# A two-layer hybrid backbone: a projection tile tied to each chunk of the forward scan, in step with the chunk, its input given two chunks later

## The chip, the cores and the metric

One Trainium2 (trn2) chip, one core. The time is that of one execution on the device, in microseconds (us). Before the change three runs gave 2162.40, 2163.49 and 2163.54 us; the median, 2163.49 us, is the figure to be forecast for the changed kernel. The profile is of one further execution. A difference of under about 0.2% (4.3 us) can't be told from no change here.

## What is computed

```python
def ssd_chunked(x, dt, a, bm, cm, h0):          # chunks of 128 tokens
    ...
    y_diag = jnp.einsum('btlsgr,btsgrp->btlgrp', cb[..., None] * decay, xdt)
    ...
    def step(h, inp):
        s, d = inp
        return h * d[..., None, None] + s, h
    h_final, h_in = lax.scan(step, h0, (jnp.moveaxis(states, 1, 0), jnp.moveaxis(chunk_decay, 1, 0)))
    ...
    y_off = jnp.einsum('btlgn,btgrpn,btlgr->btlgrp', cc, h_in, jnp.exp(a_cum))
    return (y_diag + y_off).reshape(bsz, L, G, R, P).astype(x.dtype), h_final

# in ssd_branch: both directions, gate, norm
    y = y_f + fl(y_b) + xs * d_skip.reshape(SSD_GROUPS, SSD_HPG, 1)
    y = y.reshape(bsz, L, SSD_INNER)
    return rms_norm(y * jax.nn.silu(z), norm_w), h_f, h_b

# in reference, for each of the two layers
        x = layer_norm(DEEPNORM_ALPHA * x + g_x * y_x, ln_g[layer], ln_b[layer])
```

1280 tokens (256 of context, 1024 latent) of width 1024 go through two layers in fp32. Layer 0 has two branches side by side, a bidirectional Mamba-2 scan (SSD, 16 heads of 64) and a conformer convolution. Each gives 1024 columns, and one output projection takes both, `y_x = concat(ssd, conformer) @ w_out`. Layer 1 (gMLP and windowed attention) is not touched.

## The kernel before

**Tiles and products.** Tokens go in ten tiles of 128. An fp32 product of the projection is made of three TensorE products of rounded halves: high by high, high by low, low by high. A token tile's half of the projection is 8 slices of the inner dimension, by three products, by two column halves: 48 products of 128x512, all on line L1003 (`out_mm_`, which `yield`s after each). They are called fills here.

**Two halves of the projection.** `stage_b` projects the conformer half of a token tile (its input was written to DRAM long before), adds it to the scaled residual `xl` and stores the sum in `tb_d`. `stage_a` does the SSD half later, when all of the scan's output `wt_d` is to be had. The input of either is loaded by `out_y`: a DMA from SP's queue into `yl` (L991, one buffer), then ScalarE's cast to `yh` (L158) and GpSimd's difference to `ylo` (L159, two buffers each).

**The forward scan.** Ten chunks of 128 tokens, one object `SsdFwd` each. `prep` loads the chunk's rows (`xt2`), makes the new state (`Hf`, two products on L1577) and the pair `cb` (L1590). `mix` makes the chunk's output in `t3`. For each of two groups of heads there are two products `po` with the incoming states (L1624) and, twice over, a pair `sg` of 15-row products (L1635), a mask on VectorE, an exponential on ScalarE, a product with `cbs` on GpSimd into `dec` (L1641), and eight 64-column products `yd` (L1645). `finish` gates the output with `zst` on VectorE (L1652), takes its squares on ScalarE (L1655) and `rs` and `rstd` from them on GpSimd (L1547, L1548), and turns `zst` with two sets of four transposes (L1660) for the store to `wt_d`.

**What sets the order.** The program is written in the order of the loop below, but the framework schedules it (`TileContext(nc, schedule_with_timeline_sim=True)`): each engine's instructions are put in an order of the scheduler's own, and each engine then works through its own in that order, waiting at each for what it needs. Buffers that exist once (`t3`, `zst`, `yl`, `yd`, each `sg`, the bank of `po`) must be read out before they are written again.

```python
for c in range(NT):
    S[c].mix()
    if c < NT - 1:
        S[c + 1].prep()
    S[c].finish()
    self.stage_b((c + 2) % NT, ob, w, yb_d, tb_d, grow, y0 if c == 0 else None)
```

At chunk 4 and 7 the same loop starts loads of the next weights (`wa`, 512 KB each).

Of the kernel before, what the change touches and what calls it, by code (L numbers as in the profile page):

```python
# [14 lines left out]
P = 128  # L15
# [5 lines left out]
NT = T // P  # L21
# [69 lines left out]
def run(steps):  # L91

    for _ in steps:
        pass


def h16(t):
    return t.rearrange("p (h d) -> p h d", d=64)
# [12 lines left out]
class Kern:  # L111
# [114 lines left out]
    def layer0(self):  # L226
        tc, nc, A = self.tc, self.nc, self.A
# [8 lines left out]
        yb_d = {a: dram.tile([8, P, b - a], F32, name=f"yb{a}_d") for a, b in SLICES}  # L236
# [3 lines left out]
        tb_d = dram.tile([NT, P, D], F32, name="tb_d")  # L240
# [8 lines left out]
        with e1:  # L249
            with ExitStack() as e2:  # L250
# [14 lines left out]
                wb, wl, y0 = self.inproj0(hhi, hlo, cv, xbc_d, zs_d, gs_d, dtr, vwh, yb_d, xt_d, hb_d, s0, first)  # L265
# [9 lines left out]
        ob = eo.enter_context(self.pool(name="ob", bufs=2))  # L275
        self.px = e.enter_context(self.pool(name="px", bufs=1, space=PSUM))
        g0, g1 = (ob.tile([P, D], F32, name=n, bufs=1) for n in ("g0", "g1"))
        grow = (g0, g1)
        wb0 = ob.tile([P, D], F32, name="xl", tag="xl")
        nc.sync.dma_start(wb0, A["wout0"][8])  # L280
        w = self.split_wo(wo, wb + [(0, wb0, None)], [(wl, "wb0")])
# [4 lines left out]
        with ExitStack() as e3:  # L286
            q = e3.enter_context(self.pool(name="sf", bufs=2, side="right"))
            self.rows = q.tile([111, 1280], FR, name="rows", bufs=1)
            self.rst = q.tile([111, 1280], F32, name="rst", bufs=1)
            nc.gpsimd.memset(self.rst, 0.0)  # L290
            for z in range(0, 128, 32):
                nc.sync.dma_start(self.rst[z:z + 12, :1024], A["delta"][0:12, :1024])
                nc.sync.dma_start(self.rst[z + 12:z + 15, 1024:], A["delta"][12:15, :256])
            self.mku = q.tile([P, P], mybir.dt.uint8, name="mku", bufs=1)
            nc.vector.tensor_copy(self.mku, self.tu)
            self.mmt = ("m0", "m1")
            self.ko = (*range(1, 8), 0)
            S = [SsdFwd(self, c, xbc_d, xt_d, hb_d, zs_d, wt_d, rstd, q) for c in range(NT)]
            S[0].prep()
            for c in range(NT):  # L300
                S[c].mix()
                if c < NT - 1:
                    S[c + 1].prep()
                S[c].finish()
                self.stage_b((c + 2) % NT, ob, w, yb_d, tb_d, grow, y0 if c == 0 else None)
                if c == 7:
                    wl3 = ea.enter_context(self.pool(name="wl3", bufs=1))
                    for k in range(4, 6):
                        wa.append((k, wl3.tile([P, D], F32, name=f"wa{k}", tag=f"wa{k}"), (wl3, f"wa{k}")))
                        nc.sync.dma_start(wa[k][1], A["wout0"][k])  # L310
                if c == 4:
                    for k in range(4):
                        nc.vector.tensor_copy(wa[k][1][:1, :1], self.Hf[:1, :1])
                        nc.sync.dma_start(wa[k][1], A["wout0"][k])
# [29 lines left out]
        for t in (*range(2, NT), 0, 1):  # L344
            ps = self.bank("mm")
# [638 lines left out]
        run(self.out_mm_(ps, parts or self.out_y(ob, src), w, by_k))  # L984
        return ps

    def out_y(self, ob, src):
        nc = self.nc
        oy = self.oy or ob
        y = oy.tile([P, 8, P], F32, name="yl", tag="yl", bufs=1)  # L990
        nc.sync.dma_start(y, src)  # L991
        hi = oy.tile([P, 8, P], FR, name="yh", tag="yh")
        lo = oy.tile([P, 8, P], FR, name="ylo", tag="ylo")
        self.split(y, hi, lo, self.oy is not None)
        return hi, lo
# [26 lines left out]
        nc.vector.scalar_tensor_tensor(rs[:, 1:2], mv[:, 0:1], -1.0, rs[:, 0:1], op0=ALU.mult, op1=ALU.mult)  # L1022
        return rs

    def stage_b(self, t, ob, w, yb_d, tb_d, grow, y0=None):
        nc, A = self.nc, self.A
        ts = slice(t * P, (t + 1) * P)
        x = ob.tile([P, D], F32, name="xl", tag="xl")
        nc.sync.dma_start(x, A["xc"][ts])
        a = max(x for x in yb_d if x <= t * P)  # L1030
        ps = self.out_mm(ob, yb_d[a][:, :, t * P - a:(t + 1) * P - a].rearrange("k p t -> p k t"), w, parts=y0, by_k=y0 is not None)
        g = grow[1 if t < 2 else 0]
        for f in range(2):
            fs = slice(512 * f, 512 * f + 512)
            u = ob.tile([P, 512], F32, name="u", tag="u", bufs=1)
            nc.vector.tensor_tensor(u, ps[f], g[:, fs], op=ALU.mult)
            nc.vector.scalar_tensor_tensor(x[:, fs], x[:, fs], ALPHA, u, op0=ALU.mult, op1=ALU.add)
        nc.sync.dma_start(tb_d[t], x)
# [512 lines left out]
class SsdFwd:  # L1551
# [51 lines left out]
    def mix(self):  # L1603

        K, c, q, nc = self.K, self.c, self.q, self.K.nc
        hb_d, zs_d = self.d[2:4]
        H, xt, bc, cb = self.H, self.xt, self.bc, self.cb
        zs = self.zs = q.tile([P, D], F32, name="zst", bufs=1)
        nc.sync.dma_start(zs, zs_d[c])
        t3 = q.tile([P, D], F32, name="t3", bufs=1)  # L1610
        nc.gpsimd.tensor_tensor(h16(t3), h16(xt[:, :D]), self.coef.rearrange("p g h -> p (g h)").unsqueeze(2).broadcast_to([P, 16, 64]), op=ALU.mult)
        self.t3 = t3
        for g in range(2):
            hs = slice(8 * g, 8 * g + 8)
            cs = slice(512 * g, 512 * g + 512)
            hb = None
            if c != 1:
                hb = q.tile([P, 512], F32, name="hbt", bufs=1)
                nc.sync.dma_start(hb, hb_d[c, :, cs])
            for d, S in ((1, hb), (0, H[:, cs] if H is not None else None)):  # L1620
                if S is None:
                    continue
                po = K.pp.tile([P, 512], F32, name="po", tag="m2", bufs=1)
                nc.tensor.matmul(po, bc[:, 2 + g], S, start=True, stop=True)  # L1624
                ea = K.expA[:, d, c, hs].unsqueeze(2).broadcast_to([P, 8, 64])
                t2 = q.tile([P, 512], F32, name="t2", bufs=1)
                nc.vector.tensor_tensor(h16(t2), h16(po), ea, op=ALU.mult)
                nc.vector.tensor_tensor(t3[:, cs], t3[:, cs], t2, op=ALU.add)
            yd = K.px.tile([P, 512], F32, name="yd", tag="yd", bufs=1)
            for j in range(2):  # L1630
                seg = []
                for d in range(2):
                    sg = K.px.tile([P, 512], F32, name=f"sg{d}", tag=f"sg{d}", bufs=1)
                    z = slice(64 * g + 32 * d, 64 * g + 32 * d + 15)
                    nc.tensor.matmul(sg, K.rows[z, 1024 + P * j:1024 + P * j + P], K.rows[z, 512 * j:512 * j + 512], start=True, stop=True)  # L1635
                    seg.append(sg)
                v4 = lambda t: t.rearrange("p (h t) -> p h t", h=4)
                nc.vector.copy_predicated(out=v4(seg[1]), mask=K.mku.unsqueeze(1).broadcast_to([P, 4, P]), data=v4(seg[0]))
                M = q.tile([P, 4, P], F32, name="dec", bufs=3)
                nc.scalar.activation(M.rearrange("p h t -> p (h t)"), seg[1], AF.Exp)  # L1640
                nc.gpsimd.tensor_tensor(M, M, cb[:, g * P:(g + 1) * P].unsqueeze(1).broadcast_to([P, 4, P]), op=ALU.mult)  # L1641
                for h in range(4):
                    o = 256 * j + 64 * h
                    for f in range(2):
                        nc.tensor.matmul(yd[64 * f:64 * f + 64, o:o + 64], M[:, h, 64 * f:64 * f + 64], xt[:, 512 * g + o:512 * g + o + 64], start=True, stop=True)  # L1645
            nc.vector.tensor_tensor(t3[:, cs], yd, t3[:, cs], op=ALU.add)

    def finish(self):

        K, c, q, nc = self.K, self.c, self.q, self.K.nc  # L1650
        w = self.zs
        nc.vector.tensor_tensor(w, self.t3, w, op=ALU.mult)  # L1652
        ssq = q.tile([P, 1], F32, name="ssq")
        wT = q.tile([P, D], F32, name="tmp", bufs=1)
        nc.scalar.activation(wT, w, AF.Square, accum_out=ssq)  # L1655
        K.rstd_of(ssq, self.rstd[:, c:c + 1], 1.0 / D)
        for g in range(2):
            ps = K.bank("ms")
            for k in range(4):
                nc.tensor.transpose(out=ps[:, k * P:(k + 1) * P], in_=w[:, 512 * g + k * P:512 * g + (k + 1) * P], identity=K.ident)  # L1660
            nc.scalar.copy(wT[:, 512 * g:512 * g + 512], ps)
        nc.sync.dma_start(self.d[4][c], wT.rearrange("p (k t) -> p k t", k=8))
# [19 lines left out]
```

## Time and profile before

| | |
|---|---|
| median of three runs | 2163.49 us |
| the profiled execution | 2159.51 us |
| its span, first to last instruction | 2157.5 us |
| PE (TensorE products) busy | 2050.3 us, 95% |
| PEld (weight loads, beside PE) busy | 1631.5 us, 76% |
| DVE (VectorE) busy | 1344.7 us, 62% |
| ACT (ScalarE) busy | 990.9 us, 46% |
| POOL (GpSimd) busy | 980.0 us, 45% |

The profiled execution is 2.0 us longer than its span, and 4.0 us shorter than the median. The forward scan runs from about 780 to 1058 us of the span.

### The profile page before, as it was taken

To read this page: it belongs to the slowest core of one execution; us is meant where nothing else is said; L and a number is where in the kernel's file an instruction comes from. 1 tells how busy PE (TensorE), PEld (TensorE's weight loads), DVE (VectorE), ACT (ScalarE), POOL (GpSimd) and SP (SyncE) were. 2 spreads that over 40 slices of the span, in tenths; PEclk is the share of its full clock that TensorE was granted. 3 is DMA by queue.
4 is the path that set the end of the run, shared out by engine and by line. 5 is a ranking of instruction groups with operands and counts; after the bars stand their busy time and mean duration, and the time that the engine had idled before them with its cause. 6 is when DMAs were issued, how large, how long until landed. Compare 5 with 4: busy or idle time off the path is not lost. (4 is left out here: it accounts for less than half of the span.)

```text
span 2157.5 us, 28255 instructions
## 1 busy us (share of the span) xinstructions
PE 2050.3 (95%) x10636; PEld 1631.5 (76%) x10636; DVE 1344.7 (62%) x1889; ACT 990.9 (46%) x1549; POOL 980.0 (45%) x646
## 2 busy tenths in 40 slices
PE   7999999999995999999899999999999998899896
PEld 6888888889873876665588788888777776677675
DVE  6788897758454335678776221422566766676676
ACT  7455667543362132224233333333666877655510
POOL 0198999800222235556421114823345555434562
PEclk9999999999996999999899999999999999999998
DMA  8011122235756645555343322522312111533463
GB/s 311 30 40 33 47 87 79 88 131 191 234 161 203 241 144 176 179 190 175 120 147 113 129 71 98 186 83 84 101 48 67 51 47 48 157 112 115 145 179 127
DMA packets 156976, 268.01 MB, mean 124 GB/s; under 512 B 18677, under 2 KB 97393, under 8 KB 156585
## 3 DMA queue, kind: packets, MB, share of 16 engines
q1 hardware_dynamic: 155416, 262.69, 37.0%
q0 software_dynamic: 1280, 3.26, 0.5%
q8 instruction: 83, 1.36, 0.3%
q14 instruction: 53, 0.43, 0.1%
q10 hardware_dynamic: 144, 0.26, 0.0%
HBM read 189.17 MB, written 76.94 MB: 123 GB/s over the span
## 5 line engine op out<-in xcount | busy, mean ns | idle before, releaser
L1236 POOL TENSOR_TENSOR accq<-accq,prod 128x1295 f32<-128x1295 f32 x90 | 287.7, 3197 | 33.9 <-ACT prod L1235 17.2
L171 PE MATMUL m<-hhi,wh 128*128 128x512 f32 (+1 forms) x792 | 280.9, 355 | 1.8 <-ACT th L1279 0.9
L171 PE MATMUL m<-hlo,wh 128*128 128x512 f32 (+1 forms) x792 | 280.6, 354 | 0.0
L171 PE MATMUL m<-hhi,wl 128*128 128x512 f32 (+1 forms) x792 | 280.2, 354 | 0.0
L1244 DVE SCALAR_TENSOR_TENSOR acc<-u,vwh,acc 128x1295 f32<-128x1295 f32 x150 | 235.1, 1568 | 12.9 <-ACT acc L1241 9.7
L171 PE MATMUL m<-h1hi,wh 128*128 128x512 f32 (+1 forms) x544 | 213.2, 392 | 1.7 <-ACT rb L423 1.4
L733 POOL TENSOR_TENSOR pl<-pt,ph 128x512 fp32r<-128x512 f32 x96 | 129.3, 1349 | 186.2 <-ACT ph L732 178.7
L171 PE MATMUL m<-h1lo,wh 128*128 128x512 f32 (+1 forms) x544 | 213.0, 392 | 0.0
L171 PE MATMUL m<-h1hi,wl 128*128 128x512 f32 (+1 forms) x544 | 212.1, 390 | 0.0
L1003 PE MATMUL m<-wol,yh 128*128 128x512 f32 x448 | 182.1, 406 | 1.3 <-DVE wol L956 1.1
L1003 PE MATMUL m<-woh,yh 128*128 128x512 f32 x448 | 181.4, 408 | 1.8 <-ACT yh L158 0.9
L1003 PE MATMUL m<-woh,ylo 128*128 128x512 f32 x448 | 182.0, 406 | 0.3 <-DVE ylo L159 0.3
L1235 ACT ACTIVATE prod<-u,vwh 128x1295 f32<-128x1295 f32 x90 | 124.1, 1381 | 97.9 <-POOL accq L1236 95.6
L171 PEld LDWEIGHTS m<-hhi,wh 128*128 128x128 f32 x792 | 149.7, 189 | 24.1 <-ACT th L1279 1.6
L171 PEld LDWEIGHTS m<-hhi,wl 128*128 128x128 f32 x792 | 149.7, 189 | 20.8
L171 PEld LDWEIGHTS m<-hlo,wh 128*128 128x128 f32 x792 | 149.8, 189 | 20.6
L159 POOL TENSOR_TENSOR wl<-wr,wh 128x1024 fp32r<-128x1024 f32 x33 | 81.5, 2471 | 117.2 <-ACT wh L158 95.2
L732 ACT CAST ph<-pt 128x512 fp32r<-128x512 f32 x152 | 93.1, 619 | 81.5 <-PE po L740 70.4
L740 PE MATMUL po<-ph,vs 128*66 128x512 f32 x304 | 122.0, 401 | 3.8 <-ACT yo L745 3.8
L171 PEld LDWEIGHTS m<-h1hi,wh 128*128 128x128 f32 x544 | 102.7, 189 | 22.9 <-ACT rb L423 2.0
L171 PEld LDWEIGHTS m<-h1hi,wl 128*128 128x128 f32 x544 | 102.6, 189 | 21.0 <-issue 0.2
L171 PEld LDWEIGHTS m<-h1lo,wh 128*128 128x128 f32 x544 | 102.8, 189 | 19.7
(371 smaller groups left out, 4765.6 us busy)
## 6 DMA issues: line engine op xcount, KB each, us to landing
wr<-in_wch_dram SPq DMA_DIRECT2D x69, 512.0 KB
mw<-in_modw_dram SPq DMA_DIRECT2D x24, 512.0 KB
mr<-in_modw_dram SPq DMA_DIRECT2D x16, 512.0 KB
wor<-in_wout_dram SPq DMA_DIRECT2D x16, 512.0 KB
xbc_d<-acc SPq DMA_DIRECT2D x12, 640.0 KB
xcT<-xbc_d SPq DMA_DIRECT2D x20, 320.0 KB
xt_d<-xtok SPq DMA_DIRECT2D x20, 320.0 KB
xtok<-xt_d SPq DMA_DIRECT2D x10, 640.0 KB
```

The costliest lines, as they stand in the source:

```text
L159: (nc.gpsimd if pool_lo else nc.vector).tensor_tensor(lo, src, hi.bitcast(F32), op=ALU.subtract)
L171: nc.tensor.matmul(out, x(k), y(k), start=(c == 0), stop=(c == tot - 1))
L732: nc.scalar.copy(ph, p)
L733: (nc.gpsimd if x in (0, 1, 3) else nc.vector).tensor_tensor(pl, p, ph.bitcast(F32), op=ALU.subtract)
L740: nc.tensor.matmul(po[:66], vs[:, kb, v], p[y], start=first and i == 0, stop=last and i == 2)
L1003: nc.tensor.matmul(ps[f], y[u][:, k], w[k][v][:, 512 * f:512 * f + 512], start=i + j == 0, stop=i + j == 9)
L1235: nc.scalar.activation(pr, u[:, k:k + N], AF.Copy, scale=vwh[:, i, k:k + 1])
L1236: nc.gpsimd.tensor_tensor(acc, acc, pr, op=ALU.add)
L1244: nc.vector.scalar_tensor_tensor(acc[:, :N], u[:, k:k + N], vwh[:, i, k:k + 1], acc[:, :N], op0=ALU.mult, op1=ALU.add)
```

## The change

The loop ties conformer tile i (token tile (i + 2) mod 10) to the scan. Tile 0 is given whole before chunk 0. Tile c + 1 is given with chunk c, four fills at each of the places where `mix` now yields (ahead of each `po`, each pair `sg` and each group `yd`: twelve, or ten where a state is missing), the rest behind it. The input of tile c + 2 is given with chunk c and is put behind the norm of chunk c - 1: a GpSimd copy of one element from that chunk's `rstd` into `yl` must end before the load may write there. So tile 3 waits for chunk 0, tile 4 for chunk 1, and so on to tile 9 and chunk 6; tiles 0 to 2 wait for none.

```diff
             S[0].prep()
+            run(self.stage_b(0, ob, w, tb_d, grow, y0))
+            ys = [self.stage_b_y(1, ob, yb_d)]
             for c in range(NT):
-                S[c].mix()
+                if c + 2 < NT:
+                    ys.append(self.stage_b_y(c + 2, ob, yb_d, S[c - 1] if c else None))
+                b = self.stage_b(c + 1, ob, w, tb_d, grow, ys.pop(0)) if c + 1 < NT else iter(())
+                for _ in S[c].mix():
+                    for _ in range(4):
+                        next(b, None)
+                run(b)
                 if c < NT - 1:
                     S[c + 1].prep()
                 S[c].finish()
-                self.stage_b((c + 2) % NT, ob, w, yb_d, tb_d, grow, y0 if c == 0 else None)
...
-    def out_y(self, ob, src):
+    def out_y(self, ob, src, behind=None):
         nc = self.nc
         oy = self.oy or ob
         y = oy.tile([P, 8, P], F32, name="yl", tag="yl", bufs=1)
+        if behind is not None:
+            nc.gpsimd.tensor_copy(y[:1, 0, :1], behind.last)
         nc.sync.dma_start(y, src)
...
-    def stage_b(self, t, ob, w, yb_d, tb_d, grow, y0=None):
+    def stage_b_y(self, i, ob, yb_d, behind=None):
+
+        t = (i + 2) % NT
+        a = max(x for x in yb_d if x <= t * P)
+        return self.out_y(ob, yb_d[a][:, :, t * P - a:(t + 1) * P - a].rearrange("k p t -> p k t"), behind)
+
+    def stage_b(self, i, ob, w, tb_d, grow, y):
...
-        ps = self.out_mm(ob, yb_d[a][:, :, t * P - a:(t + 1) * P - a].rearrange("k p t -> p k t"), w, parts=y0, by_k=y0 is not None)
+        ps = [self.bank("mm") for f in range(2)]
+        yield from self.out_mm_(ps, y, w, i == 0)
...
+                yield
                 po = K.pp.tile([P, 512], F32, name="po", tag="m2", bufs=1)
...
                 seg = []
+                yield
                 for d in range(2):
...
+                yield
                 for h in range(4):
...
         K.rstd_of(ssq, self.rstd[:, c:c + 1], 1.0 / D)
+        self.last = self.rstd[:1, c:c + 1]
```

In the changed program the same lines have other numbers: fills L1012, the load of `yl` L1000, `po` L1641, `sg` L1653, `yd` L1664, transposes L1680, state L1593, `cb` L1606, `rs` and `rstd` L1563 and L1564, `t3` L1627, `dec` L1659; the new copy is L999.

**Where instructions stand now.** The scheduler moves the fills among the chunks' own products. PE at the end of chunk 5, before: `zst_7684` is that chunk's gated output, and the fills around its transposes are of one and the same tile.

```order
L1003 MATMUL m1_8664<-woh7_6540,yh_8667 128x512
L1003 MATMUL m1_8664<-wol7_6541,yh_8667 128x512
L1660 MATMUL ms_7822<-cs_65,zst_7684 128x128 x4
L1660 MATMUL ms_7828<-cs_65,zst_7684 128x128 x4
L1645 MATMUL yd_7916<-xt2_7780,dec_7922 64x64 x8
L1003 MATMUL m1_8664<-woh7_6540,ylo_8668 128x512
L1003 MATMUL m1_8664<-woh0_6544,yh_8667 128x512
L1003 MATMUL m1_8664<-wol0_6545,yh_8667 128x512
```

After, at the same place, `zst_7766` is chunk 5's output and `yh_7979` the input of tile 8, whose load stands behind the norm of chunk 5:

```order
L1012 MATMUL m1_7992<-woh0_6544,ylo_7763 128x512
L1680 MATMUL ms_7963<-cs_65,zst_7766 128x128 x4
L1680 MATMUL ms_7969<-cs_65,zst_7766 128x128 x4
L1653 MATMUL sg1_8042<-rows_6579 128x512
L1664 MATMUL yd_8011<-xt2_7921,dec_8021 64x64 x8
L1653 MATMUL sg0_8086<-rows_6579 128x512
L1653 MATMUL sg1_8088<-rows_6579 128x512
L1012 MATMUL m0_8208<-woh1_6516,yh_7979 128x512
L1012 MATMUL m0_8208<-wol1_6517,yh_7979 128x512
L1012 MATMUL m1_8209<-woh1_6516,yh_7979 128x512
L1012 MATMUL m1_8209<-wol1_6517,yh_7979 128x512
```

The last fill of tile 7 now stands ahead of the transposes, and the first of tile 8 behind them and four own pieces.

PE at the end of chunk 7, before (`zst_8116`): all fills are over by then.

```order
L1645 MATMUL yd_8355<-xt2_8212,dec_8361 64x64 x8
L1660 MATMUL ms_8254<-cs_65,zst_8116 128x128 x4
L1660 MATMUL ms_8260<-cs_65,zst_8116 128x128 x4
L1635 MATMUL sg0_8402<-rows_6579 128x512
L1635 MATMUL sg1_8404<-rows_6579 128x512
L1590 MATMUL ms_8448<-bcT_8437 128x128 x2
L1635 MATMUL sg0_8418<-rows_6579 128x512
L1635 MATMUL sg1_8420<-rows_6579 128x512
```

After (`zst_8200`): `yh_8810` is the input of the first tile of `stage_a`, with that stage's weights.

```order
L1653 MATMUL sg0_8474<-rows_6579 128x512
L1680 MATMUL ms_8397<-cs_65,zst_8200 128x128 x4
L1641 MATMUL po_8440<-Hf_8144,bcT_8357 128x512
L1012 MATMUL m0_8806<-woh0_8755,yh_8810 128x512
L1012 MATMUL m1_8807<-woh0_8755,yh_8810 128x512
L1680 MATMUL ms_8403<-cs_65,zst_8200 128x128 x4
L1653 MATMUL sg1_8476<-rows_6579 128x512
L1012 MATMUL m0_8806<-wol0_8756,yh_8810 128x512
L1012 MATMUL m0_8806<-woh0_8755,ylo_8811 128x512
```

Fills now stand between the own products of chunks 7 and 8, where there were none.

POOL behind chunk 5, before (`rs_7819` and `rstdA` are that chunk's norm, `ylo_8881` belongs to `stage_a`):

```order
L1641 TENSOR_TENSOR dec_7922<-dec_7922,cbs_7806 128x512
L1547 TENSOR_SCALAR rs_7819<-ssq_7816 128x1
L1611 TENSOR_TENSOR t3_7902<-xt2_7780,coef_7812 128x1024
L1548 TENSOR_TENSOR rstdA_88<-rs_7819,mhalf_67 128x1
L1641 TENSOR_TENSOR dec_7938<-dec_7938,cbs_7806 128x512
L159 TENSOR_TENSOR ylo_8881<-yl_8878,yh_8880 128x1024
```

After, behind chunk 5 (the copy gives tile 8's buffer `yl_7976` free for its load):

```order
L1659 TENSOR_TENSOR dec_7898<-dec_7898,cbs_7722 128x512
L1563 TENSOR_SCALAR rs_7960<-ssq_7957 128x1
L1564 TENSOR_TENSOR rstdA_88<-rs_7960,mhalf_67 128x1
L999 COPY yl_7976<-rstdA_88 1x1
L1659 TENSOR_TENSOR dec_8021<-dec_8021,cbs_7947 128x512
L1627 TENSOR_TENSOR t3_7985<-xt2_7921,coef_7953 128x1024
L1659 TENSOR_TENSOR dec_8045<-dec_8045,cbs_7947 128x512
L159 TENSOR_TENSOR ylo_7980<-yl_7976,yh_7979 128x1024
```

And after, behind chunk 2, for tile 5 (`yl_7317`):

```order
L1563 TENSOR_SCALAR rs_7301<-ssq_7298 128x1
L1564 TENSOR_TENSOR rstdA_88<-rs_7301,mhalf_67 128x1
L1627 TENSOR_TENSOR t3_7326<-xt2_7262,coef_7294 128x1024
L1659 TENSOR_TENSOR dec_7362<-dec_7362,cbs_7288 128x512
L999 COPY yl_7317<-rstdA_88 1x1
```

The copy stands right behind the norm at chunk 5, and behind two larger pieces at chunk 2. What follows it in the row waits until the norm is done.

## Rows read from the trace of the kernel before

**Rows 1.** The page, section 1: busy time, share of the span, instructions.

```profile
PE 2050.3 (95%) x10636; PEld 1631.5 (76%) x10636; DVE 1344.7 (62%) x1889; ACT 990.9 (46%) x1549; POOL 980.0 (45%) x646
```

**Rows 2.** Windows: stretch, length, busy of PE, PEld, DVE, ACT, POOL, PEclk, DMA share, GB/s.

```profile
780.00:1060.00 280.00, 268.17 (x1522) 172.48 (x1521) 195.60 (x281) 90.29 (x131) 153.56 (x99) 0.97 0.52 173
```

**Rows 3.** Timeline of PE, end of the scan: start, duration, instruction, [idle before <-releaser].

```profile
1013.01 0.49 PE L1635 MATMUL sg<-rows 15*128 15x512 f32 x1
1013.43 1.09 PE L1660 MATMUL ms<-cs,zst 128*128 128x128 f32 x8
1014.45 0.69 PE L1645 MATMUL yd<-xt,dec 128*64 128x64 f32 x16
1015.07 0.74 PE L1635 MATMUL sg<-rows 15*128 15x512 f32 x2
...
1022.14 1.98 PE L1577 MATMUL ms<-tmp,xt 128*128 128x512 f32 x4
1023.97 1.02 PE L1624 MATMUL po<-Hf,bcT 128*128 128x512 f32 x2
1024.92 0.50 PE L1635 MATMUL sg<-rows 15*128 15x512 f32 x1
...
1042.72 0.49 PE L1645 MATMUL yd<-xt,dec 128*64 128x64 f32 x6
...
1052.60 1.58 PE L1624 MATMUL po<-hbt,bcT 128*128 128x512 f32 x2 [2.97 <-issue]
...
1058.41 0.50 PE L1003 MATMUL m<-woh,yh 128*128 128x512 f32 x1 [0.78 <-DVE t L1627]
```

**Rows 4.** Windows of that end, columns as in rows 2.

```profile
1052.00:1054.00 2.00, 1.40 (x2) 0.30 (x2) 1.93 (x3) 0.00 (x0) 2.00 (x2) 0.77 0.82 334
1054.00:1056.00 2.00, 1.59 (x27) 1.44 (x28) 1.74 (x3) 0.00 (x0) 0.12 (x1) 0.50 0.03 8
1056.00:1058.00 2.00, 1.63 (x13) 0.68 (x10) 0.33 (x1) 0.00 (x0) 0.00 (x0) 0.88 0.00 0
1028.00:1043.00 15.00, 13.98 (x86) 8.24 (x86) 12.00 (x22) 5.91 (x10) 7.37 (x8) 0.54 0.38 129
```

**Rows 5.** Timeline of PE: one own product among fills.

```profile
816.49 0.40 PE L1003 MATMUL m<-wol,yh 128*128 128x512 f32 x1
816.72 0.40 PE L1003 MATMUL m<-woh,ylo 128*128 128x512 f32 x1
817.05 0.49 PE L1635 MATMUL sg<-rows 15*128 15x512 f32 x1
...
817.80 0.40 PE L1003 MATMUL m<-wol,yh 128*128 128x512 f32 x1
```

**Rows 6.** Timelines of SP's queue and ACT: a load's issue, its cast.

```profile
807.50 0.38 SPq L991 DMA_DIRECT2D yl<-yb_d  x1
818.40 0.37 SPq L991 DMA_DIRECT2D yl<-yb_d  x1
...
814.60 1.05 ACT L158 CAST yh<-yl 128x1024 fp32r<-128x1024 f32 x1 [6.62 <-DMA yl<-yb_d]
823.34 1.05 ACT L158 CAST yh<-yl 128x1024 fp32r<-128x1024 f32 x1 [3.34 <-DMA yl<-yb_d]
```

**Rows 7.** Timeline of all engines: from a chunk's gate to its norm.

```profile
869.90 1.22 DVE L1652 TENSOR_TENSOR zst<-t,zst 128x1024 f32<-128x1024 f32 x1
871.15 1.06 ACT L1655 ACTIVATE tmp<-zst 128x1024 f32<-128x1024 f32 x1 [3.80 <-DVE zst L1652]
871.20 2.29 POOL L1611 TENSOR_TENSOR t<-xt,coef 128x1024 f32<-128x1024 f32 x1 [2.50 <-DVE zst L1652]
...
873.57 0.69 POOL L1547 TENSOR_SCALAR rs<-ssq 128x1 f32<-128x1 f32 x1
874.34 1.27 POOL L1641 TENSOR_TENSOR dec<-dec,cbs 128x512 f32<-128x512 f32 x1
875.57 1.01 POOL L1548 TENSOR_TENSOR rstdA<-rs,mhalf 128x1 f32<-128x1 f32 x1
```

More of the change, by code (lines that the diff above doesn't have):

```diff
@@ L1023, in ln_stats @@
         return rs
-    def stage_b(self, t, ob, w, yb_d, tb_d, grow, y0=None):
+    def stage_b_y(self, i, ob, yb_d, behind=None):
[3 more added lines that the diff above has]
+    def stage_b(self, i, ob, w, tb_d, grow, y):
         nc, A = self.nc, self.A
+        t = (i + 2) % NT
         ts = slice(t * P, (t + 1) * P)
@@ L1029, in stage_b @@
         nc.sync.dma_start(x, A["xc"][ts])
-        a = max(x for x in yb_d if x <= t * P)
-        ps = self.out_mm(ob, yb_d[a][:, :, t * P - a:(t + 1) * P - a].rearrange("k p t -> p k t"), w, parts=y0, by_k=y0 is not None)
+        ps = [self.bank("mm") for f in range(2)]
+        yield from self.out_mm_(ps, y, w, i == 0)
         g = grow[1 if t < 2 else 0]
```

## The prediction

> **What bounds the kernel now.** The page's busy shares come first: PE is busy 95% of the span, no other engine over 62% [rows 1]. That is a mean over stages, so the windows of the forward scan are read next: from 780 to 1060 us PE is busy 268.2 of 280 us, VectorE 195.6, ScalarE 90.3, GpSimd 153.6, and the DMA engines half the time [rows 2]. The scan is PE's. The 480 fills of ten tiles and the chunks' own products are as many after the change, so PE's work is the same too. What can change is the 11.8 us in which PE is idle there, the time that it works slowly, and new waits.
>
> The timeline of PE shows where that time is. Own work needs a chain over other engines (`sg`, mask, exponential, `dec`, `yd`), and fills cover it. The last fill before the end starts at 1012.69 and the next product, 1013.01, is an own one; the first of the next tile comes at 1058.41 [rows 3]. These 45.4 us hold no fill. The reader is to see two things in it: idle time (2.97 us ahead of the product at 1052.60) and a clock that falls to its lower level, 0.50 of full (1.2 of 2.4 GHz), in the second half: mean 0.54 from 1028 to 1043, when PE had had own products alone for 15 us, and 0.77, 0.50 and 0.88 in the three windows behind the 2.97 us [rows 4].
>
> **a) The end without fills: -9.7 us.** By the order, 21 `sg`, 13 groups `yd`, 10 `po`, three sets of transposes, one state pair and two `cb` pairs stand in those 45.4 us. Slots at full pace are read from one start to the next [rows 3, 5]: transposes 1.02 (1013.43 to 1014.45), `yd` 0.62 (14.45 to 15.07), state 1.83 (22.14 to 23.97), `po` 1.02 (its duration), a product of 512 columns 0.23 (816.49 to 816.72); `cb` I take at half the transposes, 0.5. So 10 x 1.02 + 13 x 0.62 + 21 x 0.23 + 3 x 1.02 + 1.83 + 1.0 = 29.0 us of work, 16.4 us lost. After the change the first `stage_a` tile has its fills in chunks 7 and 8 (the second place in the order), and the end without fills holds 6 `po`, 6 `yd`, 8 `sg` and one set of transposes, 12.7 us of work. Its last 16 pieces are, one by one, those that ran before from 1042.72 to 1058.41, 15.7 us; ahead of them stand two `po`, two `yd` and two `sg`, 3.7 us. That makes 19.4 us, 6.7 lost, and a gain of 9.7. Bounds: 6.5 us, if nearly half of the 6.9 us that the low clock cost from 1028 to 1043 (15 x 0.46 [rows 4]) is lost again elsewhere; 13, if the 3 us of idle time goes too.
>
> **b) Fewer changes between fills and own work: -7 us.** A lone `sg` between fills stretches 816.72 to 817.80, 1.08 us, for three slots of 0.23 [rows 5]: 0.4 us lost. By the order, own work is cut into 79 pieces before, 25 of them a lone `sg`, and into 57 after, 8 of them lone. For other pieces no row shows the loss plainly; I take half, 0.2 (bounds 0 and 0.4). 25 x 0.4 + 54 x 0.2 = 20.8 before, 8 x 0.4 + 49 x 0.2 = 13.0 after: 7.8, rounded down to 7. Bounds 0 and -8, since the weight loads of such pieces may lie under the products.
>
> **c) Waits for gated inputs: +15 us.** What was an early load now follows a chain. From the end of a chunk's `zst` (871.12): squares 1.1 us, `rs` 0.7, `rstd` 1.0 [rows 7], the copy of one element, for which the trace has no row. It lies between nothing and `rs`, the nearest row of such a size, 0.7; I take 0.3. Then the load. From issue to the start of the cast it took 4.9 us (818.40 to 823.34) and 7.1 (807.50 to 814.60) [rows 6]; I take 4.9, the one with the engines less full. The cast is 1.05. So 9 us from `zst` to the first fill, if nothing stands between. When PE wants it is in the order:
> - Tile 8, first place. Between chunk 5's last `yd` and its transposes stand a `po`, twelve fills and `cb`, 4.2 us, against VectorE's 1.8 (`zst` 1.22 and, by half its size, 0.6 for the sum ahead of it): PE is 2.3 late. Then transposes 1.0, `sg` 0.4, `yd` 0.6, a pair 0.5: it wants the input at 4.7 and waits 4.3.
> - Tile 3. `rs`, `rstd` and the copy stand behind `t3` (2.29) and a `dec` (1.27), as before in chunk 1, where `rstd` ended 5.5 us after `zst` [rows 7]. Ready at 12; behind the transposes stand own pieces of 7.6 us with them, at their pace (part d) 8.3 to 8.6. Wait 3.7.
> - Tile 5. The copy stands behind `t3` and `dec` (third place), but so does the `yd` that PE comes to ahead of tile 5 and that needs this `dec`; the two delays mostly coincide. About 1.
> - Tile 6, with 3.4 us of own work behind the transposes and `t3` ahead of the norm: about 2. Tile 7, with 5.9 us of own work and the four loads of `wa` (2 MB) right ahead in SP's queue: 1.8, and 2.2 more by the slower load. 4.
> - Tiles 4 and 9: 24 and 20 fills of the tile before stand between the last `yd` and the transposes, 4.6 us or more of lateness, and the rest of the chain is covered. 0. Tiles 1 and 2 wait for no chunk.
>
> Together 15. Bounds: 0, where PE is late everywhere, and 30, where every load takes 7.1 (five tiles, 11 us) and the copy 0.7, and tile 5 isn't covered. What stands behind a waiting fill on PE is the next chunk's own work, and VectorE, ScalarE and GpSimd wait for that; so a wait isn't made good by them.
>
> **d) Fill-free stretches inside the scan: +3 us.** Ahead of tiles 3, 5 and 7 the order has own work alone of 8.6, 7.6 and 6.1 us. Such work kept this pace before: 1013.01 to 1024.92 is 11.9 us [rows 3] for 10.4 us of slots (7 `sg`, 3 `yd`, 4 `po`, transposes, state), 1.14. 22.3 x 0.14 = 3. Bounds 0 and, at the pace of the whole end (45.4 for 29.0), 12.
>
> **What costs nothing.** Seven copies on GpSimd, at most 5 us in all, lie in its 126 us idle in the scan [rows 2]; without that cover the 5 us would be on the way to `dec`. The loads' number and size are the same, and so are all sums of `stage_b`.
>
> **The sum.** -9.7 - 7 + 15 + 3 = +1.3 us. The profiled execution took 2159.5 (its span and 2.0 around it); it would take 2160.8. It stood 4.0 below the median of the runs, so the forecast is 2165 us, no change that could be told (0.2%, 4.3 us).
>
> **A rule that speaks against it.** After the 2.97 us in which PE did nothing, the clock was at or on its way to the lower level for three windows: 2 x (0.23 + 0.50 + 0.12) = 1.7 us lost [rows 4]. The Trainium skill ("TensorE: Matmul & The Clock Gate", section "HAM oscillation — how this bites in real kernels") describes kernels whose products for one tile are shorter than the wait for the next tile's operands: each wait lets the clock down, and each tile begins at the lower level. The trace shows one such fall. By the row's price four waits of 3.7 us or more (tiles 3, 7, 8 and a longer 6) would add 7 us, and the sum would be +8. I leave it out of the forecast, since in the scan fills come right ahead of these waits, and before the 2.97 us own products alone had run; it belongs to the second rival.
>
> **Rivals.**
> - *The inputs are there in time* (faster). PE is later at every gate than reckoned, since own pieces themselves wait for VectorE and GpSimd. For it: they were slower than their slots in the whole end [rows 3]; the cover of tiles 4 and 9. Against: tile 8's place, with 2.5 us of own work behind the transposes. Part c falls: -13.7 us, 2150 us.
> - *The gate costs more* (slower). Place: PE at the first fill of tiles 3, 5, 6, 7, 8. The load takes 7.1, as the other row of two has it, +11, and the clock falls at four of these waits, +7. +19 us, 2183 us. For it: half the DMA share is taken already [rows 2], and rows 4. Against: the load at 818.40. It decides from c = 18 on: a mean wait of 3.7 us at the five tiles makes the kernel measurably slower.
> - *The tie doesn't take.* The code gives four fills at a step, but the order has them in clumps of up to 24 still, and the end is all that differs; if that end is then as slow as before, nothing changes: 2163 us. Against: its last rows are the same, with less ahead.
>
> **Chances.** The forecast (terms of both signs that cancel) 0.53, with a range of its own of 2154 to 2175 us (a and b at their small ends with c at 15, +8 and more; c at 5, -9). Of it 0.12 are faster, 0.27 the same, 0.14 slower by 0.2%. First rival 0.22, all faster; second 0.21, all slower; third 0.04, 0.03 the same and 0.01 faster. So faster 0.35, same 0.30, slower 0.35. The range that leaves out 2 in 10 reaches to both rivals: 2149 to 2182 us.
>
> **What would show it.** a: from the last fill to the next tile's first about 19 us, not 45, and no stretch of 15 us at half clock. b: fewer lone `sg`, with the fills between them at 0.23 us a slot. c: idle PE ahead of the first L1012 of tiles 3, 7 and 8, put down to the cast of `yh`, which itself waits for the DMA of `yl`; the load's issue behind the copy L999, 3 to 4 us behind `zst`; none at tiles 4 and 9. d: idle ahead of `yd` in the three stretches. Wrong it would be above all if a copy on GpSimd is far from 0.3 us, if the loads take 3 or 8 us, or if the clock falls inside the scan, which it hardly did before.

## The result, and the profile after

The changed kernel takes 2181.18 us (median of four runs, 2176.02 to 2184.80) against 2163.51 us (four runs of the kernel before): a ratio of 1.0083, with an interval of 1.0068 to 1.0098. It is slower by 17.7 us. The forecast was 2165 us, no change that could be told, in a range of 2149 to 2182. The time lies 0.8 us inside that range, because its upper end was drawn out to the second rival, priced at 2183 us; the forecast itself missed by 16 us. The profiled execution is the slowest of the four, 2184.80 us. The mean granted clock of the four runs goes with their time: 0.972, 0.972, 0.974 and 0.975 for 2184.80, 2183.59, 2178.77 and 2176.02 us. The spans of the two traces, 2183.1 and 2157.5 us, differ by 25.6 us.

The page of the changed kernel, section 1, answers to [rows 1]: PE is busy 11.8 us longer over as many instructions.

```profile
PE 2062.1 (94%) x10636; PEld 1641.3 (75%) x10636; DVE 1345.2 (62%) x1889; ACT 990.4 (45%) x1549; POOL 979.5 (45%) x653
```

Windows of the kernel before, and then of the changed one, each up to its last fill ahead of the end, and for the changed one the end as well (columns as in [rows 2]):

```profile
780.00:840.00 60.00, 57.23 (x296) 41.05 (x295) 35.47 (x50) 23.22 (x31) 29.93 (x19) 1.00 0.66 214
840.00:1012.00 172.00, 169.63 (x947) 108.56 (x946) 123.25 (x174) 52.35 (x76) 95.62 (x59) 1.00 0.53 176
```

```profile
780.00:840.00 60.00, 57.21 (x288) 41.32 (x286) 34.35 (x47) 20.88 (x28) 27.15 (x15) 1.00 0.57 186
840.00:1058.00 218.00, 202.21 (x1118) 128.72 (x1117) 143.48 (x206) 65.03 (x97) 118.53 (x84) 0.91 0.48 162
1058.00:1080.00 22.00, 16.55 (x129) 8.57 (x128) 16.25 (x27) 4.57 (x9) 10.56 (x8) 0.85 0.26 95
```

Up to 840 us idle time and clock are the same. From there to the last fill PE was idle 2.4 us and its clock at 1.00 before; now it is idle 15.8 us and the clock 0.91 in the mean. The groups of PE's instructions in that stretch say what it waits for (after the second bar: idle time before them, and what ended it):

```profile
L1012 PE MATMUL m<-woh,yh 128*128 128x512 f32 x128 | 57.5, 450 | 7.0 <-ACT yh L158 7.0
L1012 PE MATMUL m<-wol,yh 128*128 128x512 f32 x128 | 55.5, 433 | 2.2 <-DVE wol L963 2.1
L1653 PE MATMUL sg<-rows 15*128 15x512 f32 x62 | 26.2, 535 | 4.8 <-DVE sg L1656 4.0 <-ACT dec L1658 0.4
...
L1680 PE MATMUL ms<-cs,zst 128*128 128x128 f32 x64 | 8.8, 276 | 1.4 <-DVE zst L1671 1.4
```

7.0 us are the gated inputs, as forecast in kind; 6.2 are own pieces, nearly all of which wait for VectorE. The 2.2 us at `wol` are fills that wait for the low halves of their weights (1.1 us before). PE's timeline shows both sorts of wait, the first fills of tiles 3 (855.46) and 5 (904.93), and the end:

```profile
847.56 0.50 PE L1653 MATMUL sg<-rows 15*128 15x512 f32 x1 [1.57 <-DVE sg L1656]
...
855.46 0.80 PE L1012 MATMUL m<-woh,yh 128*128 128x512 f32 x1
...
895.13 0.49 PE L1653 MATMUL sg<-rows 15*128 15x512 f32 x1 [1.07 <-DVE sg L1656]
...
904.93 1.36 PE L1012 MATMUL m<-woh,yh 128*128 128x512 f32 x1
...
930.65 0.79 PE L1012 MATMUL m<-woh,yh 128*128 128x512 f32 x1 [3.21 <-ACT yh L158]
...
962.87 0.50 PE L1012 MATMUL m<-woh,yh 128*128 128x512 f32 x1 [2.18 <-ACT yh L158]
...
989.35 0.80 PE L1012 MATMUL m<-woh,yh 128*128 128x512 f32 x1 [1.59 <-ACT yh L158]
...
1058.08 0.40 PE L1012 MATMUL m<-woh,yh 128*128 128x512 f32 x1
1058.41 0.49 PE L1653 MATMUL sg<-rows 15*128 15x512 f32 x1
...
1072.54 1.26 PE L1641 MATMUL po<-hbt,bcT 128*128 128x512 f32 x2 [2.91 <-issue]
...
1079.30 0.80 PE L1012 MATMUL m<-woh,yh 128*128 128x512 f32 x1 [0.78 <-DVE t L1644]
```

The three waits at `yh` are those of tiles 6, 7 and 8; the first fills of tiles 3 and 5 have none. The end without fills is 20.9 us (1058.41 to 1079.30) instead of 45.4. Windows of 2 us behind such places show the clock:

```profile
896.00:898.00 2.00, 2.00 (x3) 0.42 (x2) 0.65 (x2) 0.00 (x0) 1.52 (x1) 0.50 1.00 357
930.00:932.00 2.00, 1.35 (x3) 1.16 (x4) 0.00 (x0) 1.09 (x2) 1.33 (x1) 0.50 0.99 398
964.00:966.00 2.00, 2.00 (x5) 1.10 (x5) 0.65 (x1) 0.47 (x1) 2.00 (x2) 0.53 0.35 110
988.00:990.00 2.00, 0.65 (x2) 0.55 (x3) 1.97 (x3) 1.54 (x2) 1.75 (x2) 0.50 0.95 352
```

It falls to 0.50 five times between 840 and 1058: at 848, 895, 930, 964 and 988, each time ahead of or at the first fills of one of the tiles 3, 5, 6, 7 and 8, and stays down for 4 to 12 us. By all the 2 us windows (2 x (1 - clock), summed) these falls cost 1.7, 5.1, 3.4, 3.4 and 5.1 us, 18.8 in all. At 848 and 895 no input was waited for: PE had own work alone and had waited for masks of `sg` (1.57 and 1.07 us) and, ahead of 848, for `zst` (0.87 us).

### The profile page after: what moved, and what is told of

It is laid out like the page before. It is cut to its first block, busy times and chain, and to the rows that moved or that the text cites. A ratio compares the mean times of both kernels' runs of the same rounds, so it can differ in the third digit from the quotient of the medians.

```text
span 2183.1 us, 28257 instructions
## 1 busy us (share of the span) xinstructions
PE 2062.1 (94%) x10636; PEld 1641.3 (75%) x10636; DVE 1345.2 (62%) x1889; ACT 990.4 (45%) x1549; POOL 979.5 (45%) x653
## 5 line engine op out<-in xcount | busy, mean ns | idle before, releaser
L1012 PE MATMUL m<-woh,yh 128*128 128x512 f32 x448 | 185.6, 418 | 8.8 <-ACT yh L158 7.9
L1012 PE MATMUL m<-wol,yh 128*128 128x512 f32 x448 | 184.6, 412 | 2.4 <-DVE wol L963 2.1
L1012 PE MATMUL m<-woh,ylo 128*128 128x512 f32 x448 | 185.1, 415 | 0.3 <-DVE ylo L159 0.3
L171 PEld LDWEIGHTS m<-h1hi,wl 128*128 128x128 f32 x544 | 102.6, 189 | 20.9
```

The costliest lines, as they stand in the source:

```text
L171: nc.tensor.matmul(out, x(k), y(k), start=(c == 0), stop=(c == tot - 1))
L1012: nc.tensor.matmul(ps[f], y[u][:, k], w[k][v][:, 512 * f:512 * f + 512], start=i + j == 0, stop=i + j == 9)
```

## The experiments

Three views are compared below: the ratio to runs of the kernel before that were taken along with the kernel's own (their medians lie between 2161.7 and 2163.5 us); PE's idle time in the scan (2 minus its busy time, summed over 2 us windows from 780 us to about 20 us behind the end without fills); and what the clock cost there (as above). Theory A: the time from gate to input makes the loss. Theory B: the mixing of fills and own work step by step does. Theories C and D came later, where the first ones fell.

| kernel | median, us | ratio (interval) | idle + clock, us | span less these |
|---|---|---|---|---|
| before | 2163.5 | 1 | 11.8 + 8.5 | 2137.2 |
| changed | 2181.2 | 1.0083 (1.0068 to 1.0098) | 24.0 + 23.9 | 2135.2 |
| no gate | 2167.1 | 1.0017 (1.0007 to 1.0026) | 15.4 + 12.0 | 2139.9 |
| gate, tiles whole | 2178.5 | 1.0070 (1.0054 to 1.0087) | 22.3 + 22.2 | 2135.6 |
| gate at `zst` | 2174.2 | 1.0050 (1.0034 to 1.0067) | 19.3 + 17.1 | 2130.6 |
| gate at the sum | 2175.8 | 1.0064 (1.0041 to 1.0087) | 17.5 + 25.6 | 2130.8 |
| early input | 2193.0 | 1.0137 (1.0114 to 1.0159) | 31.6 + 27.3 | 2135.2 |
| one gate | 2168.4 | 1.0026 (1.0013 to 1.0040) | 17.8 + 13.7 | 2136.9 |
| gate a chunk earlier | 2173.5 | 1.0050 (1.0035 to 1.0065) | 21.4 + 18.8 | 2132.0 |
| gate at the store | 2155.4 | 0.9967 (0.9953 to 0.9981) | 14.3 + 5.1 | 2134.4 |
| store, early input | 2185.3 | 1.0107 (1.0088 to 1.0126) | 29.7 + 15.4 | 2144.2 |
| gate at the half | 2174.2 | 1.0040 (1.0019 to 1.0060) | 20.2 + 18.8 | 2134.3 |
| mixed gates | 2165.7 | 1.0009 (0.9995 to 1.0023) | 15.8 + 10.2 | 2137.0 |
| load ahead | 2177.1 | 1.0073 (1.0059 to 1.0087) | 21.1 + 20.5 | 2132.3 |

The last column is the trace's span without the two costs. It lies between 2130.6 and 2144.2 while the spans reach from 2153.8 to 2194.1: most of what tells these kernels apart is idle PE and low clock in the scan. What differs outside the scan is in that column too.

**No gate.** The copies on GpSimd left out, the four fills per step kept.

```diff
-                    ys.append(self.stage_b_y(c + 2, ob, yb_d, S[c - 1] if c else None))
+                    ys.append(self.stage_b_y(c + 2, ob, yb_d, None))
```

> The changed kernel without the copies on GpSimd: no load waits for a norm; the four fills per step stay. Theory A (the late inputs: idle PE at the first fill of a gated tile and the fall of the clock around it make the loss): no idle time of over 1 us ahead of a fill between chunk 1 and chunk 6 and a clock of 1.00 there; but the order then has 37.8 us of own work without a fill at the end (28.4 before), at the pace of before (45.4 us for 29.0) 59 us, so 4 to 6 us more than before in the end: 2164 to 2170 us, ratio 1.000 to 1.003. Theory B (the mixing of fills and own work step by step makes own work slower): as slow as the changed kernel, 2176 us or more.

2167.08 us, inside A's numbers and far from B's. The clock was 1.00 up to 1014 us. The gate makes most of the loss, and B is out. Its order is not that of the kernel before, though: the end holds 37.8 us of own work instead of 28.4.

**Gate alone, tiles whole.**

```diff
-                for _ in S[c].mix():
-                    for _ in range(4):
-                        next(b, None)
-                run(b)
+                run(S[c].mix())
...
                 S[c].finish()
+                if c + 1 < NT:
+                    run(self.stage_b(c + 1, ob, w, tb_d, grow, ys.pop(0)))
```

> The gates stay, but the fills are given tile by tile behind the chunk's end, as before, and not four per step. By the order every engine then has the same instructions in the same order as in the changed kernel (but for branches). Theory A: 2176 to 2185 us, as the changed kernel. Theory B (the mixing in steps is what costs): back to 2163 us.

As slow as the changed kernel. The steps written in the source hardly reach an engine: in the two orders PE, VectorE and SP's queue have one instruction each at most three places elsewhere (on PE one `po`), ScalarE and GpSimd none. The scheduler makes the order from what is ready when, and of the two parts it is the gate that changes that.

**Gate at `zst`.** The gated output itself instead of its norm.

```diff
-        self.last = self.rstd[:1, c:c + 1]
+        self.last = w[:1, :1]
```

> The gate stands behind the chunk's gated output instead of its norm, a chain shorter by the squares, rs and rstd, about 3 us; the order has no stretch of own work over 4.6 us inside the scan (8.6, 7.5 and 6.1 in the changed kernel) and 7.5 us at the end. Theory A: the input is ready about 6.6 us behind the gate, PE wants it after 3 to 4 us of own work, so two or three waits of up to 3 us and fewer falls of the clock: 2160 to 2172 us. Theory B: as slow as the changed kernel, 2176 us or more, since the steps are the same.

**Gate at the last sum**, ahead of the product with `zst`; the line with `rstd` goes.

```diff
             nc.vector.tensor_tensor(t3[:, cs], yd, t3[:, cs], op=ALU.add)
+            self.last = t3[:1, 512 * g:512 * g + 1]
```

> The gate stands behind the last sum into the chunk's output, ahead of the product with zst: about 4.3 us earlier than the norm. Own work without fills: 5.5 us at most in the scan, 5.8 at the end; 59 pieces, 4 of them a lone sg. Theory A: ready about 5.4 us behind zst, and the gains in the end and by fewer pieces stay: 2150 to 2165 us, with a clock of 1.00 in most of the scan. Theory B: 2176 us or more.

2174.17 and 2175.81 us: too slow for A. At the sum the waits at `yh` had shrunk to 1.0 us, but `sg` waited 6.8 us and the clock cost 25.6. An earlier gate moves the wait from the fills to own work. So theory C: gathered fills leave own stretches, and these bring idle time and a low clock, whenever the input comes.

**Input early.** Load, cast and difference not gated; behind the norm a rewrite of one element of `yh` on VectorE (it adds 0 times the norm).

```diff
+            h = y[0][:1, 1, :1]
+            nc.vector.scalar_tensor_tensor(h, behind.last, 0.0, h.bitcast(F32), op0=ALU.mult, op1=ALU.add)
```

> The same gates (tile i behind the norm of chunk i-3), but the load, the cast and the difference go ahead of them; behind the norm stands only a rewrite of one element of yh on VectorE (0.2 to 0.3 us instead of the 6.6 us of copy, load and cast). The fills are gathered behind the gates as in the changed kernel: own stretches without fills of 5.7, 6.0, 8.9 and, at the end, 12.2 us. Theory A (the time from gate to input makes the loss): no idle PE of over 1 us ahead of first fills, a clock of 1.00 in the scan, and the gain in the end stays: 2150 to 2160 us. Theory C (own stretches without fills between the gathered fills bring the clock down, whenever the input comes): three or four falls of 3 to 4 us each stay: 2165 to 2178 us.

2193.03 us, the slowest, and outside both. The run isn't clean: the rewrite waits in VectorE's row and the masks wait behind it. The group of `sg` (780 to 1050 us) shows it:

```profile
L1660 PE MATMUL sg<-rows 15*128 15x512 f32 x66 | 31.5, 562 | 8.6 <-DVE sg L1663 6.9 <-DVE t L1672 1.3 <-ACT dec L1665 0.2
```

**One gate**, and **gates a chunk earlier**: the last argument of `stage_b_y` in the two kernels.

```diff
-S[c - 1] if c else None
+S[c - 1] if c == 6 else None
...
-S[c - 1] if c else None
+S[c - 2] if c > 1 else None
```

> Only tile 8 is gated, behind the norm of chunk 5; the other copies are left out. The order has one stretch of 24.0 us of own work ahead of tile 8 and 13.8 us at the end. Theory A: one wait of up to 4 us and one fall, and half of the gain in the end: 2160 to 2166 us. Theory C: the 24 us bring the clock down as the 28.4 us at the end of the kernel before did (10 to 14 us lost there), and the end loses 7 to 9: 2163 to 2172 us. The clock from chunk 1 to chunk 4 is 1.00 by both.

> Each gate stands behind the norm of the chunk before (tile i behind chunk i-4), so inputs have a chunk's time, some 30 us, more. The order has own stretches of 10.2 us in the scan and 17.2 at the end. Theory A: no wait at a first fill, a clock of 1.00 but for the end, and half of the gain in the end: 2153 to 2161 us. Theory C: the clock falls in the 10.2 us and at the end: 2160 to 2168 us.

2168.43 us with one gate is C's range, a little above A's; the clock stayed at 1.00 up to 950 us and fell three times from there to 990. 2173.46 us with the earlier gates is slower than either had it: four falls. One (966 to 977) lies in the 10.2 us stretch. The longest (904 to 924) is at the first fills of tile 6, behind own work with a wait of 1.40 us for a mask, and that tile's input came 2.44 us late, where A expected no wait.

**Gate at the store.** The gate stands behind ScalarE's copy of the transposed output, later than the norm.

```diff
+        self.last = wT[:1, 512:513]
         nc.sync.dma_start(self.d[4][c], wT.rearrange("p (k t) -> p k t", k=8))
```

> Each gate stands behind the copy of the chunk's transposed output instead of its norm. Own stretches of 8.6, 6.3, 6.4, 5.2 and 6.4 us, the last at the end. Theory A: the chain is as long or up to 2 us longer, so PE waits at more first fills than in the changed kernel, in all over 7.0 us: 2180 to 2192 us. Theory C: one fall for each of five stretches: 2175 to 2187 us.

2155.38 us: faster than the kernel before, where both theories had 2175 us or more. Windows and groups of PE (840 to 1050 us) of this run:

```profile
840.00:860.00 20.00, 17.39 (x100) 8.96 (x99) 12.30 (x16) 6.16 (x10) 11.51 (x9) 0.74 0.57 187
880.00:960.00 80.00, 76.48 (x460) 48.56 (x460) 56.76 (x97) 22.83 (x36) 50.78 (x36) 1.00 0.59 196
960.00:1040.00 80.00, 76.53 (x475) 49.30 (x474) 60.90 (x87) 30.88 (x43) 47.37 (x32) 1.00 0.51 168
```

```profile
L1012 PE MATMUL m<-woh,yh 128*128 128x512 f32 x128 | 54.9, 430 | 0.0
...
L1653 PE MATMUL sg<-rows 15*128 15x512 f32 x70 | 25.7, 508 | 2.5 <-DVE sg L1656 1.8 <-ACT dec L1658 0.4
```

One fall of the clock instead of five, and no wait at a first fill. The order of this kernel has 7.5 to 12.0 us of work between a chunk's transposes and its tile; the changed one has 2.3 to 7.5. From that came theory D: what counts is the chain from the transposes to the input, less the work that PE's order has between them.

**Three tests of D**: the store's gate with the input early (the rewrite on VectorE as above), the gate at the first half's copy, and tile 3 behind the sum with the rest behind the store. The edits of the last two, against the gate at the store:

```diff
-        self.last = wT[:1, 512:513]
+        self.last = wT[:1, :1]
...
+            self.last = t3[:1, 512 * g:512 * g + 1]
...
-        self.last = wT[:1, 512:513]
+        if c:
+            self.last = wT[:1, 512:513]
```

> Inputs loaded and cast early, and the fills of tile i held behind the copy of chunk i-3's transposed output by the rewrite of one element of yh. Theory D (what costs is the shortfall: the time from the start of a chunk's transposes on PE to the input, less the work that PE's order has between them; the clock then falls where PE idles): the order has 1.5 to 2.7 us there, and the chain (transposes, two copies, rewrite) takes 2.2 to 3 us by the run with the gate behind the store, 4.7 at the first chunk: shortfalls of 0.3 to 1 us and one of 3, in all 4 to 7 us (17.6 in the changed kernel), 2152 to 2162 us. Theory C (own stretches without fills): 6.4 and 12.2 us remain, 2158 to 2166 us. If early input by itself is what hurt in the run with the norm's gate: 2180 us or more.

> The gate stands behind the copy of the first half of the transposed output instead of the second. The order has 7.5, 9.3, 8.5, 6.2, 9.4, 12.0 and 6.8 us between a chunk's transposes and its tile; the chain takes 8.8 to 10 us, 0.6 less than in the run with the gate behind the store. Theory D: shortfalls 2.4, 0, 1.3, 2.7, 0.6, 0 and 2.4, 9.4 us in all, between the changed kernel (17.6) and the run with the gate behind the store (6.7): 2157 to 2167 us. Theory C: own stretches of 8.6, 8.5, 9.4 and 5.2 us, four falls: 2165 to 2180 us.

> Tile 3 is gated behind the last sum of chunk 0, all others behind the copy of the transposed output. The order has 2.3, 10.4, 9.1, 12.0, 10.1, 9.4 and 12.0 us between transposes and tile, and own stretches of 7.6, 6.4, 5.4 and 6.4 us; it has 74 pieces instead of 63. Theory D: shortfall 3 at tile 3, about 1.5 in all elsewhere: 2150 to 2158 us, faster than the kernel before. Theory C: four falls, 2160 to 2175 us.

None came out as D had it: 2185.25, 2174.19 and 2165.65 us. The first has the fault of the rewrite again (9.0 us of waits of `sg` for the mask). The second lies between the two kernels that it was put between, but 7 us above its range. The third has no wait at `yh` left, as D said, and two falls of the clock (10.2 us): the same time as the kernel before. D puts the kernels in order by their waits at first fills (shortfalls of 17.6, 9.4, 6.7 and 4.5 us; waits of 7.0, 2.6, 0 and 0), but not by their time.

**Load ahead of the gate.** Nothing on VectorE this time.

```diff
-        if behind is not None:
-            nc.gpsimd.tensor_copy(y[:1, 0, :1], behind.last)
         nc.sync.dma_start(y, src)
+        if behind is not None:
+            z = oy.tile([P, 1], F32, name="yz", tag="yz", bufs=2)[:1]
+            nc.gpsimd.tensor_scalar(z, behind.last, 0.0, None, op0=ALU.mult)
+            nc.gpsimd.tensor_tensor(y[:1, 0, :1], y[:1, 0, :1], z, op=ALU.add)
```

> The changed kernel with the load ahead of the gate: the input is in yl long before, and behind the norm of chunk i-3 stand only two one-column operations on GpSimd, which rewrite one element of yl, and the cast (1.05 us), instead of copy, load (4.3 to 7.7 us) and cast. Nothing is added to VectorE. The order has 4.0, 2.1, 5.7, 3.5, 4.4, 2.1 and 2.0 us between a chunk's transposes and its tile, and own stretches of 5.5, 5.7 and 12.2 us. Theory A (the load behind the gate is the cost) and theory D (shortfall: chains of the changed kernel less 5.3 us are 6.1, 0.7, 5.7, 2.5, 3.6, 0.5 and 0; shortfall 2.1 in all): 2150 to 2161 us, idle ahead of first fills under 3 us (7.0 in the changed kernel). If instead tying tiles to chunks costs whatever the load does (own pieces wait for VectorE where no fill may stand between): 2166 us or more, with idle time ahead of sg and yd and the clock falling there.

2177.05 us, so A and D fall, and the last sentence of what was expected holds. Groups of PE from 840 to 1054 us:

```profile
L1014 PE MATMUL m<-woh,yh 128*128 128x512 f32 x128 | 55.9, 438 | 0.4 <-ACT yh L158 0.4
...
L1655 PE MATMUL sg<-rows 15*128 15x512 f32 x62 | 26.0, 523 | 4.3 <-DVE sg L1658 3.4 <-ACT dec L1660 0.6
L1666 PE MATMUL yd<-xt,dec 128*64 128x64 f32 x466 | 21.0, 237 | 3.8 <-POOL dec L1661 3.7
```

The 7.0 us of waits for inputs are down to 0.4, and `yd` and `sg` wait 8.1 instead of 5.1: own work takes on about half of what the inputs no longer cost. The clock costs 18.8 us in this stretch, as much as in the changed kernel. The timeline at one of these places, the end of chunk 2:

```profile
893.33 0.40 PE L1014 MATMUL m<-woh,ylo 128*128 128x512 f32 x1
893.56 1.03 PE L1682 MATMUL ms<-cs,zst 128*128 128x128 f32 x8
893.76 0.69 DVE L1054 TENSOR_TENSOR u<-m,g 128x512 f32<-128x512 f32 x1 [0.59 <-PE m L1014]
...
894.49 1.82 DVE L1055 SCALAR_TENSOR_TENSOR xl<-xl,u 128x512 f32<-128x512 f32 x1
...
896.24 0.68 DVE L1658 COPY_PREDICATED sg<-mku,sg 128x512 f32<-128x512 uint8 x1
...
896.97 0.50 PE L1655 MATMUL sg<-rows 15*128 15x512 f32 x1 [1.94 <-DVE sg L1658]
```

The tile ends just ahead of the chunk's transposes, so its closing sums (`u`, `xl`, 2.5 us) stand on VectorE ahead of the mask that the next chunk's own work needs, and no fill may run: the next tile is gated. The clock falls from 898 on. In the changed kernel the row at 895.13 is the same place.

## Why the forecast came out as it did

Against the two traces, in idle time and low clock:
- **a, the end.** -4.6 us, not -9.7. The end has the length worked out, nearly (20.9 us, 19.4 forecast), but its clock fell as well and stayed low into the next fills: idle 5.5 and clock 5.1 us, against 6.7 and 8.5 before. In the forecast's own measure, length less work, the end lost 8.2 us (20.9 for 12.7) instead of 16.4, where 6.7 were forecast; that measure leaves out the fills at half pace behind it.
- **b, fewer changes.** Not settled: -2 us by the difference of the table's last column, about -6 if what differs outside the scan is taken out of it; -7 was forecast. Outside the scan the changed trace has 1.6 us more idle PE and 2.6 us more low clock than the trace before, 1.7 of that ahead of 780 us, where the scan has not begun. Two kernels with nearly the same order, the changed one and that with tiles whole, still differ by 1.5 us by this count, and no run tried the term by itself. Counted as in the later runs, the orders hold 76 and 62 pieces instead of 79 and 57 (the lone `sg` are right), which makes the term 6.2 instead of 7.8.
- **c, gated inputs.** 7.0 us, not 15. The chain was as worked out: for tile 6 (its `zst` ends at 919.88) `rstd` at 923.65, copy 0.18, load 5.6 from issue to cast, ready at 930.6, 10.7 us behind `zst`; by the forecast's terms, with `t3` (2.29) ahead of the norm, 10.2. From issue to cast it was 4.1 to 5.7 us at six tiles; at tile 5 it was 7.7, where the profile puts the last 2.0 us of ScalarE's wait down to `dec` on GpSimd and not to the load. But PE came later than reckoned to tiles 3, 5, 7 and 8: it waited 0, 0, 2.2 and 1.6 us there, where 3.7, 1, 4 and 4.3 were forecast, and 3.2 at tile 6 instead of 2. At tile 3 the input was ready 11.5 us behind `zst` (12 forecast), and own work with waits and a low clock of its own took as long. Tiles 4 and 9 waited for nothing, as forecast.
- **d, own stretches.** 13.4 us more idle time between 840 and the last fill; less c, 6.4 us, where 3 were forecast; 1.1 of it are the fills that wait for `wol`.
- **The clock.** +18.8 us, not in the sum. This is the step that failed: "I leave it out of the forecast, since in the scan fills come right ahead of these waits". Fills had ended only 1 to 7 us ahead of these waits, and the clock fell at all five places all the same, at two of them without a wait for an input. The price of a fall, 1.7 us from [rows 4], was low too: 3.8 in the mean, since the lower level lasted 4 to 12 us: through own work at 848 and 895, and through fills at 930, 964 and 988 (slots of 0.43 us instead of 0.23).

-4.6 - 2.0 + 13.4 + 18.8 = 25.6 us, the difference of the spans; the -2.0 is what is left over. What the medians differ by, 17.7, is less, since the trace of before is of an execution 4.0 us under its kernel's median and that of after of one 3.6 us over.

The second rival's time was right and its make-up only in part: it had 11 us from slow loads, which didn't come, and 7 from the clock, which cost 18.8. That the two come to nearly the same time is luck. The rule of the Trainium skill ("TensorE: Matmul & The Clock Gate", section "HAM oscillation — how this bites in real kernels") should have had more weight: tiles whose products begin at the lower clock behind a wait are what the rows at 930 and 988 show, and at 964 the clock fell four fills later. With the price of a fall from [rows 4] that rule made the sum +8. The trace goes beyond it: at 848 and 895 the clock fell with no wait for a DMA. The third rival was half right: the four fills a step do next to nothing, but the gate moves the order.

Shown are these: the gate makes most of the loss, with or without the steps (ratio 1.0017 without the gate, 1.0070 with it and without the steps); the loss is idle PE and low clock in the scan; the load behind the gate isn't needed for it (1.0073), since own work waits more and the clock falls as much. That the tile's closing sums on VectorE are what own work waits for is read from timelines and was not tried by itself. Open is why the gate at the store keeps the clock up with own stretches as long (6.3, 6.4, 5.2 and 6.4 us; its one fall is at the 8.6) as in kernels that lose it; and no run took the low clock and the idle time apart.

## What to carry to other kernels

Where a scheduler sets the order, a data dependence moves work and the order of the source may not: compare the orders before pricing. Filler work held back by a gate is taken from where it covered something; look at what the covered work waits for at the gate, and price the clock's fall there as well as the wait. Moving the gate from the norm to the copy of the transposed output, 0 to 4 us behind the norm in the trace, gave another order and turned 0.8% slower into 0.3% faster here; moving it ahead of the norm left 0.5 to 0.6% slower. So its place is worth trying rather than reckoning.

## What was not expected of the hardware

The clock fell with PE busy nearly all the time. One wait of 1.07 us among own products (895.13) stood between fills at full pace and ten us at 0.50; in the 20 us from 886 to 906 PE was idle 1.2 us. A wait of that length does not always do it. With the gate at the store PE waited longer among own products twice (timeline of PE, from 880 to 1040, where the clock was 1.00):

```profile
927.95 1.98 PE L1593 MATMUL ms<-tmp,xt 128*128 128x512 f32 x4 [1.38 <-POOL tmp L1586]
...
1003.93 1.98 PE L1593 MATMUL ms<-tmp,xt 128*128 128x512 f32 x4 [1.39 <-POOL tmp L1586]
```

Eight of the fourteen kernels lost 17 us or more in the scan to the clock alone, over three times what the fastest lost (5.1). The clock also goes with the spread of the changed kernel's runs: 0.003 of 2180 us is 6.5 us, of the 8.8 that lie between its shortest and longest.
